# VectorE's add of two weight quarters, moved behind the low parts of the next up product

## The chip, the cores and the metric

The kernel runs on one core of one Trainium2 chip. The metric is the time of one execution on the device, in microseconds; the median of three runs is 2432.49 us (2432.47 to 2432.61). A core has five engines that run side by side, each through its own list of instructions in order, and that wait for each other through semaphores: TensorE (PE: matmuls, and PEld, the loads of the stationary operand), VectorE (DVE), ScalarE (ACT), GpSimd (POOL) and SyncE (SP). Here SyncE and GpSimd mostly issue transfers (DMA). The order in which each engine's instructions stand is fixed when the program is built.

## The reference

A decoder trunk of two layers on 256 tokens with 2048 features. Layer 0 mixes with a gated linear recurrence (HGRN2), layer 1 with an attention whose keys decay. Behind each mixer stands the MLP, which this change touches, and then a gated embedding:

```python
def sq_relu_mlp(u, w_up, w_down):
    hid = jax.nn.relu(u @ w_up)
    return (hid * hid) @ w_down

h = h + sq_relu_mlp(rms_norm(h, mlp_norm[layer]), w_mlp_up[layer], w_mlp_down[layer])
```

`w_up` is 2048 x 8192, `w_down` 8192 x 2048, all in float32. A changed order of work changes none of it.

## The kernel before

Each float32 factor is split into a high part, rounded to the 32-bit format that TensorE multiplies at full rate, and a low part, the rest. A product is three matmuls: high by high, high by low, low by high. Activations are split once. Weights come from memory into one of three buffers `raw` (1 MB each, `load_slab`, loaded by SyncE), and `split` makes the parts, 1024 columns at a time: ScalarE casts the high part `whi` (line 113), VectorE subtracts for the low part `wlo` (line 114). There are four buffers of each, used in turn; one is free when TensorE has done with it. `split` notes its last subtraction under the name "lo" in `order`, and `behind(ins, "lo")` tells the scheduler that `ins` must stand behind that subtraction on its engine, without a wait.

The MLP (`mlp`) goes through the 8192 hidden features in eight blocks b of 1024. `up(b, i)` makes 128 of them: 48 matmuls of 256 columns into a PSUM tile `ps`, with the slab of `w_up` as the weights; then ReLU and scale on VectorE (`scr`, line 304), a square on ScalarE (line 306), and the split of the result into `hid` (lines 237, 238). For the second four of a block, sums and differences of quarters of the hidden tile are made too (`sf`, lines 317 to 322).

`down(b)` multiplies a block with `w_down` by a scheme of seven products in place of eight: the hidden tile and the weights are cut in two by two quarters (features by tokens, features by columns), sums of quarters are multiplied, and the results `acc` are combined at the end. It does this for two sets of columns. The larger set's products are `p1` to `p7`; the smaller set's are `r1` to `r7`, with the running weight sum in the buffer `chq` (128 x 1536), and two products, `m0` and `m1`, cover the remaining columns. In the smaller set `r1` uses a quarter and `r5` the sum with a second one that the transfer adds. `r3` adds the buffer `cq` (line 436). `r6` multiplies that sum. `r2` loads another quarter into a `raw` buffer, multiplies it, and adds it to `chq` (line 429): this is the smaller set's last weight sum. `r4` splits and multiplies the result, and `r7` uses `cq`. The products `p` and `r` are 9 or 12 matmuls of 512 columns into PSUM, `pp` when the result is then added to `acc` by VectorE (line 338; copied by ScalarE in the first block, line 336), `pn` when a bank (`nbank`) gathers it over all blocks.

The list in line 467 sets the order of the products: for each block b from 1, eight `up(b, n)` with the products of `down(b - 1)` between them, ending in `up r6 r2 up r4 r7`. `Line` chains all matmuls of the MLP in that order on TensorE. The other engines' lists are laid out by a scheduler that places each instruction by an estimate of when its inputs are there, except where `behind` binds it. Behind the last block the results are combined (lines 477, 480), transposed (line 508) and added to the residual; the last block's second half is multiplied plainly, with weights loaded on line 514.

Of the kernel before, what the change touches and what calls it, by code (L numbers as in the profile page):

```python
# [14 lines left out]
ALU = mybir.AluOpType  # L15
# [20 lines left out]
def yoco_kernel(ctx, tc, a, out):  # L36
    nc = tc.nc
# [50 lines left out]
    def load_slab(src, n, parts, before=None):  # L88

        raw = wp.tile([P, D], F32, name="raw", tag="raw", bufs=3)  # L90
        m = n // parts
        if not before:
            nc.sync.dma_start(raw[:, :n], src)
        got = []
        for i in range(parts):
            r = raw[:, i * m : (i + 1) * m]
            if before:
                before[i]()
                nc.sync.dma_start(r, src[:, i * m : (i + 1) * m])
            got.append(split(r, m))  # L100
        return got
# [3 lines left out]
    def behind(ins, name):  # L105

        tc.add_manual_dep(ins.ins, order[name].name, mybir.DependencyInfo(mybir.DependencyClass.NoSync, mybir.DependencyReason.DATA), reason="order")

    def split(r, m, to=None, **dims):
        hi = wp.tile([P, 1024], F32R, name="whi", tag="whi", bufs=4)  # L110
        lo = wp.tile([P, 1024], F32R, name="wlo", tag="wlo", bufs=4)
        h_, l_ = (x[:, :m].rearrange(to, **dims) if to else x[:, :m] for x in (hi, lo))
        nc.scalar.copy(h_, r)  # L113
        order["lo"] = nc.vector.tensor_tensor(l_, r, h_.bitcast(F32), op=ALU.subtract).ins  # L114
        return hi, lo

    def wk(pair, k, lo):
        return pair[lo][:, k * P : (k + 1) * P]
# [17 lines left out]
    def mm_split(pairs, act, kcs=KC, off=0, ps=None, mm=nc.tensor.matmul):  # L136
        if ps is None:
            ps = psm.tile([P, T], F32, name="ps", tag="mm")
        for k in range(kcs):
            kk = k + off  # L140
            pair, kl = pairs[kk // 8], kk % 8
            st, sp = k == 0, k == kcs - 1
            mm(ps, wk(pair, kl, 0), act[:, k, 0, :], start=st, stop=False)  # L143
            mm(ps, wk(pair, kl, 0), act[:, k, 1, :], start=False, stop=False)  # L144
            mm(ps, wk(pair, kl, 1), act[:, k, 0, :], start=False, stop=sp)  # L145
        return ps
# [103 lines left out]
    def mlp(layer, u, stats, slots, u2, g2, pool, pps):  # L250
# [21 lines left out]
        chq = pool.tile([P, 1536], F32, name="chq", tag="chq", bufs=1)  # L272
# [15 lines left out]

        scr = pool.tile([P, 3 * T], F32, name="scr", tag="scr", bufs=1)
        squares = pool.tile([P, 2, T], F32, name="sqrs", tag="sqrs", bufs=1)  # L290
        def up(b, i):

            n = i // 2 + i % 2 * 4
            if n == 0:
                f = slot_flat(slots[b % 2], f"hid{layer}_{b}", 0 if b == NBL - 1 else 24)
                nf = f[:, : 8 * 2 * T].rearrange("p (k w t) -> p k w t", w=2, t=T)
                sf = f[:, 8 * 2 * T :].rearrange("p (j f w t) -> p j f w t", j=4, f=4, w=2)
                hid[b] = nf, sf
            nf, sf = hid[b]
            ps = mm_split(load_slab(a["w_up"][layer, b * 8 + n], D, 2), u, mm=line)  # L300
            if not rs:
                rs.append(stats.rstd())
            t = scr[:, :T]
            nc.vector.scalar_tensor_tensor(t, ps, 0.0, rs[0], op0=ALU.max, op1=ALU.mult)
            s = squares[:, i % 2, :]
            nc.scalar.activation(s, t, AF.Square)
            plain_split(nf, n, s)
            if b == NBL - 1:
                return
            if n < 4:  # L310
                return

            x = scr[:, T:].rearrange("p (f t) -> p f t", f=4)
            a11, a12 = (squares[:, i, :P] for i in range(2))
            a21 = squares[:, 0, P:].unsqueeze(1).broadcast_to([P, 2, P])
            both = squares.rearrange("p i t -> p (i t)").rearrange("p (g t) -> p g t", t=P)[:, 0::3]
            nc.vector.tensor_tensor(x[:, 0:2], a21, both, op=ALU.subtract)
            nc.vector.tensor_tensor(x[:, 2], a11, x[:, 1], op=ALU.subtract)
            nc.vector.tensor_tensor(x[:, 3], a12, x[:, 2], op=ALU.subtract)
            o = sf[:, n - 4]  # L320
            nc.scalar.copy(o[:, :, 0, :], x)
            nc.vector.tensor_tensor(o[:, :, 1, :], x, o[:, :, 0, :].bitcast(F32), op=ALU.subtract)
# [44 lines left out]
        def down(b):  # L367

            nf, sf = hid[b]

            def plain(half, tok):
                return lambda j: tuple(nf[:, 4 * half + j, w, tok * P : (tok + 1) * P] for w in range(2))

            def form(i):
                return lambda j: tuple(sf[:, j, i, w, :] for w in range(2))

            def one(name, op, pairs):
                o = psm.tile([P, 512], F32, name="pp", tag="mm")
                product(o, op, pairs, True)
                into(name, o)  # L380

            last = b == NBL - 2
            add = dict(accum_op=ALU.add)

            def p1():
                load(nc.gpsimd, cA, quarter(b, 0, 0))
                load(nc.gpsimd, cB, quarter(b, 1, 4))
                pairs = halves(cA)
                load(nc.gpsimd, cA, quarter(b, 0, 4), **add)
                one("1", plain(0, 0), pairs)  # L390

            def p3():
                one("3", form(S4), halves(cB))

            def p2():
                one("2", plain(1, 0), loaded(quarter(b, 1, 0)))

            def p5():
                one("5", form(S1), halves(cA))

                for i in range(2):
                    v, w = (x.rearrange("p (n k c) -> p k n c", n=4, k=4)[:, 2 * i : 2 * i + 2] for x in (cA, cB))
                    nc.vector.tensor_tensor(v, v, w, op=ALU.add)
                load(nc.gpsimd, cB, quarter(b, 0, 4), **add)

            def p7():
                one("7", form(S3), halves(cB))
                load(nc.gpsimd, cq, quarter(b, 1, 12, f=fr))

            def p6():  # L410
                pairs = halves(cA)
                load(nc.gpsimd, cA, quarter(b, 1, 0), **add)
                one("6", form(S2), pairs)

            def p4():
                one("4", plain(1, 1), halves(cA))

            def r1():
                load(nc.gpsimd, chq, quarter(b, 0, 8, f=fr))
                pairs = chunks(chq, 3)  # L420
                load(nc.gpsimd, chq, quarter(b, 0, 12, f=fr), **add)
                one("r1", plain(0, 0), pairs)

            def r2():
                r = raw_tile()[:, :1536]
                load(nc.sync, r, quarter(b, 1, 8, f=fr))
                product(nbank[0][0], plain(1, 0), chunks(r, 3), False, last)

                behind(nc.vector.tensor_tensor(chq, chq, r, op=ALU.add), "lo")  # L429

            def r5():
                one("r5", form(S1), chunks(chq, 3))

            def r3():
                product(nbank[1][0], form(S4), chunks(cq, 3), False, last)
                behind(nc.vector.tensor_tensor(chq, chq, cq, op=ALU.add), "lo")
                load(nc.gpsimd, cq, quarter(b, 0, 12, f=fr), **add)

            def r6():
                one("r6", form(S2), chunks(chq, 3))  # L440

            def r4():
                product(nbank[0][1], plain(1, 1), chunks(chq, 3), False, last)

            def r7():
                one("r7", form(S3), chunks(cq, 3))

            def m(q):

                raw = raw_tile()[:, :1024]  # L450
                load(nc.sync, raw, quarter(b, q, 8, 8, fm))
                hi, lo = split(raw, 1024)
                for c in range(2):
                    cols = slice(c * 512, (c + 1) * 512)
                    for t in range(2):

                        product(nbank[c][t], lambda j: plain(q, t)(3), [(hi[:, cols], lo[:, cols])], b == q == 0, last and q == c == t == 1)

            return dict(p1=p1, p2=p2, p3=p3, p4=p4, p5=p5, p6=p6, p7=p7, r1=r1, r2=r2, r3=r3,
                        r4=r4, r5=r5, r6=r6, r7=r7, m0=lambda: m(0), m1=lambda: m(1))  # L460

# [379 lines left out]
    late = ctx.enter_context(tc.tile_pool(name="late", bufs=1))  # L841
# [245 lines left out]
```

## Time and profile before

| what | value |
| --- | --- |
| median of three runs | 2432.49 us |
| the profiled execution, its own time | 2432.98 us |
| its span (first to last instruction) | 2431.2 us |
| TensorE: matmuls / weight loads | 2404.9 us (99%) / 2285.2 us (94%) |
| VectorE / ScalarE / GpSimd busy | 1937.2 us (80%) / 1474.8 us (61%) / 157.9 us (6%) |
| granted clock of TensorE, mean | 0.997 |
| one block of an MLP (sum to sum) | 83.76 us |

In rows of the profile a number such as L114 is a line of the kernel; `out<-in` gives tiles by name. A timeline row gives start, length, engine, line, operation, tiles, shapes and how many were merged; the bracket behind it gives how long the engine had been idle before it and what ended that. A row of waits gives the total, how often and the longest. Rows of one engine may overlap a little, since the next instruction starts while the end of the last one is still on its way. In a merged row of two, the length goes from the first one's start to the last one's end.

### The profile page before, as it was taken

How to read it: one execution, taken by the hardware profiler on the slowest of the kernel's cores; microseconds unless marked ns; L12 is line 12 of the kernel's file. 1: busy time of each engine (PE TensorE's matmuls, PEld its weight loads, DVE VectorE, ACT ScalarE, POOL GpSimd, SP SyncE). 2: the span in 40 equal slices, each digit the busy share in tenths (PEclk: the TensorE clock that was granted, in tenths of full speed). 3: DMA queues.
4: the chain of work that ended last, by engine and by line, in shares of the span. 5: the costliest groups of instructions: out<-in, count | busy, mean ns of one | idle time of the engine just before them, and what ended most of it. 6: DMA issues, size and time to landing. Idle time of an engine off the chain costs nothing.

```text
span 2431.2 us, 43771 instructions
## 1 busy us (share of the span) xinstructions
PE 2404.9 (99%) x17898; PEld 2285.2 (94%) x17898; DVE 1937.2 (80%) x2914; ACT 1474.8 (61%) x2224; POOL 157.9 (6%) x201
## 2 busy tenths in 40 slices
PE   9999999999999999999999999999999999999998
PEld 8999999999999999899999999999999999989998
DVE  7897797678888888889874566667888888888976
ACT  6666575566666666656664555556666666665664
POOL 1000000001110111110000000000011011111000
PEclk9999999999999999999999999999999999999999
DMA  6554545578888887886555655557888888788653
GB/s 243 175 182 174 186 179 208 196 235 250 231 226 243 239 230 234 251 213 230 189 184 183 206 178 179 180 196 246 237 232 235 241 246 219 237 246 225 226 191 122
DMA packets 148985, 518.07 MB, mean 213 GB/s; under 512 B 9136, under 2 KB 59888, under 8 KB 111408
## 3 DMA queue, kind: packets, MB, share of 16 engines
q1 hardware_dynamic: 95200, 382.62, 44.2%
q0 software_dynamic: 52288, 130.62, 23.6%
q8 instruction: 140, 2.29, 0.4%
q10 hardware_dynamic: 1296, 2.03, 0.2%
q14 instruction: 61, 0.50, 0.1%
HBM read 508.91 MB, written 6.32 MB: 212 GB/s over the span
## 4 chain that ended last, share of the span: by engine, by line
PE 96%; DVE 2%; issue 1%; ACT 0%; DMA 0%; POOL 0%; DVEq 0%; POOLq 0%
PE ps L131 29%; PE pp L131 15%; PE ps L143 12%; PE ps L145 12%; PE ps L144 12%; PE pst L131 7%; PE pn L131 6%; DVE wlo L114 1%; DVE chq L429 0%; ACT whi L113 0%; PE pu L143 0%; PE pu L144 0%; PE pu L145 0%; DVE accr L338 0%; PE pa L741 0%
## 5 line engine op out<-in xcount | busy, mean ns | idle before, releaser
L113 ACT CAST whi<-raw 128x1024 fp32r<-128x1024 f32 (+2 forms) x742 | 763.3, 1033 | 667.9 <-PE ps L144 280.1
L114 DVE TENSOR_TENSOR wlo<-raw,whi 128x1024 fp32r<-128x1024 f32 (+2 forms) x742 | 886.6, 1200 | 329.2 <-ACT whi L113 323.5
L131 PE MATMUL ps<-u_m,whi 128*128 128x256 f32 x4096 | 707.3, 276 | 0.0
L131 PEld LDWEIGHTS ps<-u_m,whi 128*128 128x128 f32 x4096 | 626.0, 188 | 8.7
L131 PE MATMUL ps<-u_m,wlo 128*128 128x256 f32 x2048 | 566.4, 277 | 9.0 <-DVE wlo L114 8.8
L131 PEld LDWEIGHTS ps<-u_m,wlo 128*128 128x128 f32 x2048 | 384.6, 188 | 11.8 <-DVE wlo L114 11.8
L131 PE MATMUL pp<-whi,hid 128*128 128x512 f32 x1120 | 364.1, 390 | 0.0
L113 ACT CAST whi<-chain 128x1024 fp32r<-128x1024 f32 x224 | 221.1, 997 | 137.6 <-PE ps L131 89.2
L114 DVE TENSOR_TENSOR wlo<-chain,whi 128x1024 fp32r<-128x1024 f32 x224 | 256.7, 1156 | 28.4 <-ACT whi L113 26.8
L131 PEld LDWEIGHTS pp<-whi,hid 128*128 128x128 f32 x1120 | 210.2, 188 | 41.3
L131 PE MATMUL pp<-wlo,hid 128*128 128x512 f32 x560 | 218.5, 390 | 0.0
L143 PE MATMUL ps<-u_a,whi 128*128 128x256 f32 x768 | 213.6, 278 | 0.0
L145 PE MATMUL ps<-u_a,wlo 128*128 128x256 f32 x768 | 211.9, 276 | 0.0
L144 PE MATMUL ps<-u_a,whi 128*128 128x256 f32 x768 | 211.9, 276 | 0.0
L131 PE MATMUL pn<-whi,hid 128*128 128x512 f32 x476 | 158.2, 390 | 0.0
L283 POOL DMA_DIRECT2D chain<-in_w_down x98 | 104.0, 1061 | 749.7 <-DVE wlo L114 302.3
L143 PEld LDWEIGHTS ps<-u_a,whi 128*128 128x128 f32 x768 | 144.3, 188 | 0.2
L144 PEld LDWEIGHTS ps<-u_a,whi 128*128 128x128 f32 x768 | 144.3, 188 | 0.2
L145 PEld LDWEIGHTS ps<-u_a,wlo 128*128 128x128 f32 x768 | 144.2, 188 | 0.1
L143 PE MATMUL ps<-u_p,whi 128*128 128x256 f32 x512 | 141.2, 276 | 0.0
L145 PE MATMUL ps<-u_p,wlo 128*128 128x256 f32 x512 | 140.9, 275 | 0.0
L144 PE MATMUL ps<-u_p,whi 128*128 128x256 f32 x512 | 140.9, 275 | 0.0
(294 smaller groups left out, 4712.7 us busy)
## 6 DMA issues: line engine op xcount, KB each, us to landing
raw<-in_w_up SPq DMA_DIRECT2D x128, 1024.0 KB, 5.6
chain<-in_w_down POOLq DMA_DIRECT2D x70, 1024.0 KB, 9.4
raw<-in_w_ain SPq DMA_DIRECT2D x48, 1024.0 KB, 4.8
raw<-in_w_pg SPq DMA_DIRECT2D x32, 1024.0 KB, 4.8
raw<-in_w_down SPq DMA_DIRECT2D x30, 1024.0 KB, 5.4
chq<-in_w_down POOLq DMA_DIRECT2D x28, 768.0 KB, 6.5
chain<-in_w_down POOLq DMA_DIRECT2D x28, 768.0 KB, 6.5
raw<-in_w_vf SPq DMA_DIRECT2D x20, 832.0 KB, 4.4
```

What stands on the lines that cost most here:

```text
L113: nc.scalar.copy(h_, r)
L114: order["lo"] = nc.vector.tensor_tensor(l_, r, h_.bitcast(F32), op=ALU.subtract).ins
L131: ins = nc.tensor.matmul(*args, **kw).ins
L143: mm(ps, wk(pair, kl, 0), act[:, k, 0, :], start=st, stop=False)
L144: mm(ps, wk(pair, kl, 0), act[:, k, 1, :], start=False, stop=False)
L145: mm(ps, wk(pair, kl, 1), act[:, k, 0, :], start=False, stop=sp)
L283: eng.dma_start(dst.rearrange("p (n f) -> p n f", f=src.shape[-1]), src, **kw)
```

## The change

The sum on line 429 is no longer issued inside `r2`. `r2` puts it on a list, `late`, and the next `up` issues it once the up product's slab has been split and its matmuls have been issued. It is still bound behind the last low part, which now is the second low part of that up's slab. `r4`, which reads the sum, still comes after that up.

```diff
         scr = pool.tile([P, 3 * T], F32, name="scr", tag="scr", bufs=1)
         squares = pool.tile([P, 2, T], F32, name="sqrs", tag="sqrs", bufs=1)
+        late = []
+
         def up(b, i):
...
             ps = mm_split(load_slab(a["w_up"][layer, b * 8 + n], D, 2), u, mm=line)
+            while late:
+                late.pop()()
             if not rs:
                 rs.append(stats.rstd())
...
                 product(nbank[0][0], plain(1, 0), chunks(r, 3), False, last)
 
-                behind(nc.vector.tensor_tensor(chq, chq, r, op=ALU.add), "lo")
+                late.append(lambda: behind(nc.vector.tensor_tensor(chq, chq, r, op=ALU.add), "lo"))
```

Four lines come in ahead, so line 429 is line 433 in the changed kernel, and 304, 338, 317, 508 are 308, 342, 321, 512. How VectorE's list stands between `r2` and `r7` in the second block of the first MLP: before,

```order
L114 TENSOR_TENSOR wlo<-raw,whi 128x512
L429 TENSOR_TENSOR chq<-chq,raw 128x1536
L238 TENSOR_TENSOR hid_2_7569<-sqrs,hid_2_7569 128x256
L338 TENSOR_TENSOR accr_7442<-accr_7442,pp 128x512
L114 TENSOR_TENSOR wlo<-raw,whi 128x1024 x2
L114 TENSOR_TENSOR wlo<-chq,whi 128x1024
L114 TENSOR_TENSOR wlo<-chq,whi 128x512
L114 TENSOR_TENSOR wlo<-chain,whi 128x1024
L304 SCALAR_TENSOR_TENSOR scr<-ps,rstd 128x256
L114 TENSOR_TENSOR wlo<-chain,whi 128x512
L317 TENSOR_TENSOR scr<-sqrs 128x256
```

and in the changed kernel (the 128x512 low part from `raw` is the end of `r2`'s weights, the two 128x1024 ones are the up slab's; `chq` is `r4`'s, `chain` is `r7`'s):

```order
L114 TENSOR_TENSOR wlo<-raw,whi 128x512
L238 TENSOR_TENSOR hid_2_7569<-sqrs,hid_2_7569 128x256
L342 TENSOR_TENSOR accr_7442<-accr_7442,pp 128x512
L114 TENSOR_TENSOR wlo<-raw,whi 128x1024 x2
L433 TENSOR_TENSOR chq<-chq,raw 128x1536
L114 TENSOR_TENSOR wlo<-chq,whi 128x1024
L114 TENSOR_TENSOR wlo<-chq,whi 128x512
L308 SCALAR_TENSOR_TENSOR scr<-ps,rstd 128x256
L114 TENSOR_TENSOR wlo<-chain,whi 128x1024
L114 TENSOR_TENSOR wlo<-chain,whi 128x512
L321 TENSOR_TENSOR scr<-sqrs 128x256
```

The sum now stands behind the up slab's two low parts, and the ReLU of that up (`scr`) now stands ahead of both low parts of `r7`. In the last block of each MLP the scheduler also places the first four transposes of the results elsewhere on TensorE. Before, they stand inside `r7` (`pp`), behind `r4` (`pn`):

```order
L131 MATMUL pn_6166<-whi,hid_6_11005 128x512
L131 MATMUL pp<-whi,hid_6_11005 128x512
L508 MATMUL ptr<-ident,acc_7231 128x128
L508 MATMUL ptr<-ident,acc_7254 128x128
L508 MATMUL ptr<-ident,acc_7231 128x128
L508 MATMUL ptr<-ident,acc_7254 128x128
L131 MATMUL pp<-wlo,hid_6_11005 128x512
```

and in the changed kernel behind the last up (`ps`), ahead of `r4`:

```order
L131 MATMUL ps<-u_m_5112,wlo 128x256
L512 MATMUL ptr<-ident,acc_7231 128x128
L512 MATMUL ptr<-ident,acc_7254 128x128
L512 MATMUL ptr<-ident,acc_7231 128x128
L512 MATMUL ptr<-ident,acc_7254 128x128
L131 MATMUL pn_6166<-whi,hid_6_11005 128x512
L131 MATMUL pn_6166<-wlo,hid_6_11005 128x512
```

The four transposes pass the nine matmuls of `r4` and the first of `r7`. In that block VectorE's list also has a final sum (line 477 before) between the two low parts of the up slab, and two more (lines 480 and 477) between the moved sum and `r4`'s low parts. The lists of SyncE and GpSimd are the same in both kernels.

## The prediction

> **The bound.** I read the page first, then TensorE's waits, then single rows around one of the moved sums. The page's first part (busy time, share of the span, instructions) and the chain that ended last, by engine:
>
> ```profile
> PE 2404.9 (99%) x17898; PEld 2285.2 (94%) x17898; DVE 1937.2 (80%) x2914; ACT 1474.8 (61%) x2224; POOL 157.9 (6%) x201
> PE 96%; DVE 2%; issue 1%; ACT 0%; DMA 0%; POOL 0%; DVEq 0%; POOLq 0%
> ```
>
> TensorE is the bound, and VectorE (DVE) has 2% of the chain: some 49 us through which the chain runs over VectorE, though TensorE was busy during most of it. What counts is how long TensorE stood. The waits of TensorE, products and weight loads (total us, times, longest), the summed rows of line 429, and one block of the first MLP from one sum to the next (length, then busy time of PE, PEld, DVE, ACT, POOL):
>
> ```profile
> PE ps L131 <- DVE wlo L114: 8.8, 12, 0.7
> PEld ps L131 <- DVE wlo L114: 11.8, 14, 0.9
> ...
> L429 DVE TENSOR_TENSOR chq<-chq,raw x14: 1750/1751/1753, 599.3 to 2258.2; 128x1536 f32<-128x1536 f32 x14
> ...
> 682.50:766.26 83.76, 83.03 (x556) 76.01 (x556) 73.76 (x94) 52.16 (x67) 9.46 (x9) 1.00 0.84 236
> ```
>
> Fourteen weight loads of an up product waited for a low part, and there are fourteen sums on line 429. In a block of 83.76 us TensorE is idle for 0.73 us, and that is one of these waits. So the block holds one hole, and the rest of it is full at a granted clock of 1.00.
>
> The hole, in the second block, in order of time on TensorE (r6 is pp, r2 pn, up ps; then r4 pn, r7 pp, the next up), with the weight load that waits:
>
> ```profile
> 681.16 0.40 PE L131 MATMUL pp<-whi,hid 128*128 128x512 f32 x1
> ...
> 683.00 0.39 PE L131 MATMUL pp<-whi,hid 128*128 128x512 f32 x1
> ...
> 685.26 0.39 PE L131 MATMUL ps<-u_m,whi 128*128 128x256 f32 x2
> 686.38 0.19 PEld L131 LDWEIGHTS ps<-u_m,wlo 128*128 128x128 f32 x1 [0.93 <-DVE wlo L114]
> 686.39 0.38 PE L131 MATMUL ps<-u_m,wlo 128*128 128x256 f32 x1 [0.73 <-DVE wlo L114]
> ...
> 691.75 0.40 PE L131 MATMUL pn<-whi,hid 128*128 128x512 f32 x1
> ...
> 693.80 0.39 PE L131 MATMUL pp<-whi,hid 128*128 128x512 f32 x1
> ...
> 695.84 0.39 PE L131 MATMUL ps<-u_m,whi 128*128 128x256 f32 x2
> ```
>
> And VectorE and ScalarE (ACT) in the same place:
>
> ```profile
> 681.90 0.69 DVE L114 TENSOR_TENSOR wlo<-raw,whi 128x512 fp32r<-128x512 f32 x1
> 682.51 1.75 DVE L429 TENSOR_TENSOR chq<-chq,raw 128x1536 f32<-128x1536 f32 x1
> 684.18 0.42 DVE L238 TENSOR_TENSOR hid<-sqrs,hid 128x256 fp32r<-128x256 f32 x1
> 684.51 0.68 DVE L338 TENSOR_TENSOR accr<-accr,pp 128x512 f32<-128x512 f32 x1
> 685.11 2.36 DVE L114 TENSOR_TENSOR wlo<-raw,whi 128x1024 fp32r<-128x1024 f32 x2
> 687.38 1.82 DVE L114 TENSOR_TENSOR wlo<-chq,whi 128x1024 fp32r<-128x1024 f32 x2
> ...
> 691.95 0.42 DVE L304 SCALAR_TENSOR_TENSOR scr<-ps,rstd 128x256 f32<-128x256 f32 x1 [0.53 <-PE ps L131]
> ...
> 682.27 0.41 ACT L237 CAST hid<-sqrs 128x256 fp32r<-128x256 f32 x1
> 682.74 2.01 ACT L113 CAST whi<-raw 128x1024 fp32r<-128x1024 f32 x2
> 684.78 1.57 ACT L113 CAST whi<-chq 128x1024 fp32r<-128x1024 f32 x2
> ...
> 693.32 2.01 ACT L113 CAST whi<-raw 128x1024 fp32r<-128x1024 f32 x2
> ```
>
> VectorE runs without a gap from 681.90 to the low parts. The high part of the up slab is cast from 682.74, yet its low part starts only at 685.11, behind the sum (1.67 us from its start to the next start), the low part of the hidden tile (0.33) and the accumulation of r6 (0.60).
>
> **Its price.** The up product takes 691.75 - 685.26 = 6.49 us. An undisturbed one, and the ends of the one in the first block (where r6 is copied by ScalarE and no accumulation stands in front):
>
> ```profile
> 668.31 5.48 PE ps L131 x48
> ...
> 602.09 0.39 PE L131 MATMUL ps<-u_m,whi 128*128 128x256 f32 x2
> ...
> 607.99 0.40 PE L131 MATMUL pn<-whi,hid 128*128 128x512 f32 x1
> ```
>
> So a hole costs 6.49 - 5.48 = 1.01 us in a block with the accumulation (twelve, six in each MLP), and 5.90 - 5.48 = 0.42 us in each MLP's first block (two). Sum: 12 x 1.01 + 2 x 0.42 = 12.96 us. That is all that can be won here.
>
> **The change.** No instruction is added or removed: the fourteen sums of 1.75 us stay. Three things move.
>
> *The low parts go ahead of the sum.* In the new order VectorE has, behind the 0.69 us low part of r2: hidden low part, accumulation, two low parts of up, the sum. The hidden low part can start when its cast ends, 682.27 + 0.41 = 682.68, so at about 682.71. The accumulation needs r6's last matmul, 683.00 + 0.39 = 683.39; the hand-over took 0.04 us at the hole (685.11 + 1.23 = 686.34 to 686.38), so it starts at 683.43. The first low part follows 0.60 later at 684.03, ends at 685.26 and is seen at 685.30. The waiting weight load was ready at 686.38 - 0.93 = 685.45. So the hole closes with 0.15 us to spare. That is thin; a shortfall of 0.1 us in each of twelve blocks would cost 1.2 us, plus a little for the restart. Bounds: nothing is left of the hole, or half of it (0.5 us, if the accumulation gets its PSUM bank later than I think). I take 0.02 a block, near the computed end: 0.3 us in all. In the first blocks there is no accumulation and the margin is wider. The low part's own lower limit, the cast's end at 682.74 + 1.05, does not bind.
>
> *The sum, and what hangs on it, comes later.* The second low part starts 1.13 us behind the first (2.36 - 1.23), the sum at 686.30; it ends at 688.05 instead of 684.26. Then ScalarE's cast of chq (about 1.05) to 689.13, and its low part to 690.39. r4 now starts at 691.75 - 1.01 = 690.74 and wants the first low part with its second matmul, 0.23 later (2.05 us for nine), at 690.97. Cover: 0.58 us, where it was 3.4 us before (687.38 + 1.23 against 691.75 + 0.23). If the cover went, each 0.1 us beyond it costs 1.4 us over fourteen blocks.
>
> *Behind that on VectorE,* the ReLU of up (scr) now stands ahead of r7's two low parts. It waits for the end of up, 691.95 - 1.01 = 690.94, when VectorE is just free; r7's first low part runs 691.27 to 692.50, wanted at 693.80 - 1.01 + 0.23 = 693.02. Then 0.69, 0.42, and the next up's first low part, whose cast (693.32 - 1.01) ends at 693.36: about 693.40 to 694.63, wanted at 695.84 - 1.01 + 0.19 = 695.02. Margins of 0.5 and 0.4 us; no new hole.
>
> **Queues.** The sum is the last reader of r2's raw tile, so the load that takes that slot (the weights of the second up after it) goes out later. SyncE's wait for the sum, the issue, its cast, and the time to landing of raw loads in this block (660 to 720 us) and in the whole span:
>
> ```profile
> SPq L93 <- DVE chq L429: 94.8, 12, 7.9
> SPq L514 <- DVE chq L429: 15.2, 2, 7.6
> ...
> 684.33 3.50 SPq L93 DMA_DIRECT2D raw<-in_w_up  x2
> ...
> 698.69 1.06 ACT L113 CAST whi<-raw 128x1024 fp32r<-128x1024 f32 x1 [0.94 <-PE ps L131]
> ...
> DMA to landing us min/median/max: 3.9/7.4/7.9
> ...
> DMA to landing us min/median/max: 3.6/4.8/12.1
> ```
>
> Issue moves from 684.33 to 688.12; with 7.4 to 7.9 us it lands by 696.0, and the cast is due at 697.68. TensorE needs that slab at 694.83 + 5.48 + 2.73 = 703.04 (an up and the twelve matmuls of p1), so landing by 700.7 is enough (1.05 of cast, 1.23 of low part). Cost zero. The loads queued behind it on SyncE (one at about 687.5 in the old run) shift by under a microsecond. GpSimd's next chq load waits for the end of r4's low parts, which moves from 687.38 + 1.82 = 689.20 to about 690.98; its data is wanted two ups and two products after r7, as r1. Cost zero.
>
> **Last blocks.** The last block of each MLP has final sums between, and four transposes move ahead of r4:
>
> ```profile
> 1105.20 0.38 PE L131 MATMUL ps<-u_m,wlo 128*128 128x256 f32 x1 [0.73 <-DVE wlo L114]
> 1106.20 0.68 DVE L477 TENSOR_TENSOR accr<-accr,accr 128x512 f32<-128x512 f32 x1
> 1108.54 0.68 DVE L480 TENSOR_TENSOR accr<-pn,accr 128x512 f32<-128x512 f32 x1
> 1112.87 0.60 PE L508 MATMUL ptr<-ident,acc 128*128 128x128 f32 x4
> ```
>
> It is the second block plus 418.81 us. One 0.60 us step goes between the two low parts, so the sum ends at 1107.46 and the cast at 1108.54; two steps of 0.60 follow the sum, and chq's first low part ends at 1109.81. The transposes read PSUM bank pn00 freed by the L480 step (about 1108.1), so they run at 1109.55 for 0.35 us, and r4 wants its low part at 1110.13. No wait. Their cost is only moved. The two L514 loads behind the sum feed products that start some 10 us later. Cost zero, with 1 us either way.
>
> **Sum.** 2432.49 - 12.96 + 0.3 = 2419.8 us. The profiled execution took 2432.98 with a span of 2431.2, so 1.8 us lie around the span and it stands 0.5 above the median; its span should become about 2418.5.
>
> **Rivals.**
>
> *A: VectorE's steps do not overlap.* If each step began only when the one before had ended, the margins shrink: first low part seen at 685.38 (still in time), chq's at 690.66, the ReLU ends at 691.77, r7's low part is 0.02 late, and the next up's ends at 695.34, 0.36 late. Twelve times 0.36 is 4.3: 2423.8 us. Against it: 684.18 + 0.42 is 684.60, and the next row starts at 684.51; the rows overlap by 0.09 throughout. The Trainium skill, "VectorE: DVE Perf Modes", section "The DRAIN you can't avoid", has it this way: a next step does not begin until the pipe is empty. By that rule this rival would hold; these rows speak for earlier starts. 7%.
>
> *B: the accumulation is late and half the hole stays:* 12 x 0.5 = 6 us back, 2425.8. For it: no row here shows an accumulation waiting on pp, only the 0.04 of other hand-overs. 5%.
>
> *C: the low parts are held by their ring of four buffers, not by the sum,* and the hole stays: 2432.5. Against it: their buffers were r6's, last read by TensorE before 683.4, and VectorE had no idle time ahead of 685.11. The Trainium skill, "Perfetto Trace Analysis", section "Identifying the Most-Contended Engine", says that a gap which repeats can mean too few buffers; by that rule nothing would change, but the rows name VectorE's queue. 4%.
>
> *D, slower: the later load becomes the bound.* Place: the raw slot that the sum frees. From 12.6 us to landing (700.7 - 688.12) TensorE waits, from 13.6 the block is slower than before. At 15 us: 14 x 2.4 - 13 = 20.6 us, 2453. Against it: 7.9 here, 12.1 the longest anywhere. 4%.
>
> **Numbers.** Forecast 80%: 2419.8, between 2418.4 (another 0.1 a block that the holes cost in restarts) and 2422. A ends within 2424.0, which I take as the upper end. About 0.2%, 4.9 us, is what this measurement can tell from no change; A and B still lie beyond it. Faster 80 + 7 + 5 = 92%, less 1 for a shortfall that I do not see; within it C and that one, 5%; slower D, 4%.
>
> **Signs.** Right: TensorE's waits for low parts in the MLP blocks gone, a block of 82.75 us instead of 83.76, the accumulation's row at about 1.1 us earlier than now, chq's low part ending within 0.6 us before r4. Wrong: a wait on the first or second matmul of r4 or r7 (the sum too late), on the next up's low part (A), or a raw cast that waits for a DMA (D).

## The result

The changed kernel takes 2419.90 us in the median of five runs (2419.56 to 2420.65), the kernel before, beside it, 2432.47 us (2431.91 to 2432.61): a ratio of 0.9949, 95% interval 0.9935 to 0.9964. That is 12.6 us less. Its profiled span is 2418.2 us, 13.0 us under the old one.

The page of the changed kernel, busy time and chain by engine:

```profile
PE 2401.8 (99%) x17898; PEld 2284.9 (94%) x17898; DVE 1934.8 (80%) x2914; ACT 1472.1 (61%) x2224; POOL 157.9 (7%) x201
PE 99%; DVE 0%; DMA 0%; ACT 0%; issue 0%; POOL 0%; DVEq 0%; POOLq 0%
```

VectorE's 2% of the chain are gone. The weight loads of the low parts, in the groups by line (busy, mean ns, idle time before and its releaser), of before:

```profile
L131 PEld LDWEIGHTS ps<-u_m,wlo 128*128 128x128 f32 x2048 | 384.6, 188 | 11.8 <-DVE wlo L114 11.8
```

and of the changed kernel, with a block of the first MLP from sum to sum:

```profile
L131 PEld LDWEIGHTS ps<-u_m,wlo 128*128 128x128 f32 x2048 | 384.6, 188 | 0.0
...
685.88:768.64 82.76, 82.76 (x557) 75.94 (x556) 73.57 (x94) 51.95 (x66) 9.45 (x9) 1.00 0.85 238
```

All fourteen waits are gone, and TensorE is busy for the whole 82.76 us of the block, which was 83.76 before. The first matmul of the first MLP and the first of the embedding behind it, before:

```profile
484.92 0.39 PE L131 MATMUL ps<-u_m,whi 128*128 128x256 f32 x2
...
1161.98 0.28 PE L143 MATMUL pu<-pt,whi 128*128 128x256 f32 x1
```

and in the changed kernel:

```profile
484.91 0.39 PE L131 MATMUL ps<-u_m,whi 128*128 128x256 f32 x2
...
1155.48 0.28 PE L143 MATMUL pu<-pt,whi 128*128 128x256 f32 x1
```

This MLP went from 677.06 to 670.57 us, 6.49 less. The second one, between the same two instructions, went from 677.08 to 670.57. So both together give 13.0 us, and the rest of the program is as it was.

The second block of the changed kernel, TensorE, in order of time:

```profile
680.75 0.40 PE L131 MATMUL pp<-whi,hid 128*128 128x512 f32 x1
...
684.85 0.39 PE L131 MATMUL ps<-u_m,whi 128*128 128x256 f32 x2
684.96 0.19 PEld L131 LDWEIGHTS ps<-u_m,wlo 128*128 128x128 f32 x1
685.08 0.28 PE L131 MATMUL ps<-u_m,wlo 128*128 128x256 f32 x1
...
690.33 0.40 PE L131 MATMUL pn<-whi,hid 128*128 128x512 f32 x1
690.33 0.19 PEld L131 LDWEIGHTS pn<-wlo,hid 128*128 128x128 f32 x1
690.56 0.39 PE L131 MATMUL pn<-wlo,hid 128*128 128x512 f32 x1
```

and VectorE, ScalarE and SyncE there:

```profile
683.01 0.69 DVE L342 TENSOR_TENSOR accr<-accr,pp 128x512 f32<-128x512 f32 x1 [0.28 <-PE pp L131]
683.61 2.35 DVE L114 TENSOR_TENSOR wlo<-raw,whi 128x1024 fp32r<-128x1024 f32 x2
685.88 1.75 DVE L433 TENSOR_TENSOR chq<-chq,raw 128x1536 f32<-128x1536 f32 x1
688.81 1.83 DVE L114 TENSOR_TENSOR wlo<-chq,whi 128x1024 fp32r<-128x1024 f32 x2 [1.18 <-ACT whi L113]
690.55 0.42 DVE L308 SCALAR_TENSOR_TENSOR scr<-ps,rstd 128x256 f32<-128x256 f32 x1
690.89 1.82 DVE L114 TENSOR_TENSOR wlo<-chain,whi 128x1024 fp32r<-128x1024 f32 x2
...
693.04 1.23 DVE L114 TENSOR_TENSOR wlo<-raw,whi 128x1024 fp32r<-128x1024 f32 x1
...
697.27 1.06 ACT L113 CAST whi<-raw 128x1024 fp32r<-128x1024 f32 x1 [1.11 <-PE ps L131]
...
685.99 2.00 SPq L93 DMA_DIRECT2D raw<-in_w_up  x2
```

The block runs 0.41 us earlier than in the old trace (680.75 against 681.16). The first low part now ends at 683.61 + 1.23 = 684.84, and its weight load runs at 684.96 without a wait. VectorE's new idle time, 1.18 us for ScalarE's cast of chq, stands where nobody waits for it.

### The profile page after: what moved, and what is told of

Its sections match the earlier page's. It is cut to its first block, busy times and chain, and to the rows that moved or that the text cites. A ratio compares the mean times of both kernels' runs of the same rounds, so it can differ in the third digit from the quotient of the medians.

```text
span 2418.2 us, 43787 instructions
## 1 busy us (share of the span) xinstructions
PE 2401.8 (99%) x17898; PEld 2284.9 (94%) x17898; DVE 1934.8 (80%) x2914; ACT 1472.1 (61%) x2224; POOL 157.9 (7%) x201
## 4 chain that ended last, share of the span: by engine, by line
PE 99%; DVE 0%; DMA 0%; ACT 0%; issue 0%; POOL 0%; DVEq 0%; POOLq 0%
PE ps L131 29%; PE pp L131 16%; PE ps L143 12%; PE ps L145 12%; PE ps L144 12%; PE pst L131 8%; PE pn L131 7%; PE pu L145 0%; PE pu L144 0%; PE pu L143 0%; PE pa L745 0%; PE ptr L512 0%; PE pl L951 0%; DMA lbl<-in_lb 0%; PE ptp L974 0%; DVE h L1024 0%
## 5 line engine op out<-in xcount | busy, mean ns | idle before, releaser
L113 ACT CAST whi<-chq 128x1024 fp32r<-128x1024 f32 x112 | 92.2, 837 | 99.2 <-PE ps L131 74.1
L143 PE MATMUL ps<-u_p,whi 128*128 128x256 f32 x512 | 141.2, 276 | 0.0
```

## The experiments

The kernel before stood beside every one (2432.5 to 2432.8 us). Where a fraction of a microsecond counts, the length of one block, sum to sum, is compared; the whole time also holds the first stage, whose length until the first MLP differs between the traces by up to 1.4 us (483.9 to 485.3), and what stands behind the second MLP, which differs by up to 0.9 us (111.9 to 112.8).

**The accumulation moved in the sum's place** (on the kernel before, with the list `late` of the change):

```diff
     else:
-        nc.vector.tensor_tensor(acc[name], acc[name], ps, op=ALU.add)
+        def add():
+            return nc.vector.tensor_tensor(acc[name], acc[name], ps, op=ALU.add)
+        if name == "r6":
+            late.append(lambda: behind(add(), "lo"))   # issued in the next up, as in the change
+        else:
+            add()
```

> The kernel before, with the sum left in front, but the accumulation of r6 (0.60 us from start to start) moved behind the up slab's low parts in its place. Queue theory: in the twelve blocks that have an accumulation the hole shrinks by 0.60 us, from 1.01 to about 0.4; the two first blocks keep 0.42. 12 x 0.60 = 7.2 us less than the kernel before: about 2425.2 us, and fourteen waits of about 0.3 us are left. Theory that the sum itself does it (its data, its raw buffer or its load): no change, 2432.5 us. Buffer theory: no change.

Measured: 2425.27 us, ratio 0.9969 (0.9958 to 0.9981), 7.2 us less. Its wait rows and a block:

```profile
PEld ps L131 <- DVE wlo L114: 4.7, 14, 0.3
...
681.52:764.70 83.18, 83.05 (x556) 76.02 (x555) 73.75 (x94) 52.16 (x67) 9.46 (x9) 1.00 0.84 237
```

Fourteen waits of 0.3 us are left, and a block is 0.58 us shorter. The sum stands where it stood, the buffers, its data and its load are as before, and the hole shrinks by the time of the step that left the front. This rules out both the buffers and the sum's data as the cause: what counted was VectorE's time in front of the low parts.

**The front doubled, and half of that** (on the kernel before; the up slab's low parts are kept behind both steps):

```diff
-                behind(nc.vector.tensor_tensor(chq, chq, r, op=ALU.add), "lo")
+                behind(nc.vector.tensor_tensor(chq, chq, chq, op=ALU.max), "lo")   # 768 columns in the second
+                s = nc.vector.tensor_tensor(chq, chq, r, op=ALU.add)
+                behind(s, "lo")
+                order["front"] = s.ins      # later low parts are put behind this
```

> The kernel before, with a second step of the same size as the sum (maximum of chq with itself, which leaves chq as it is) on VectorE ahead of the sum, and both ahead of the up slab's low parts. Queue theory (a hole is the time that VectorE's list takes in front of the low parts): each of the fourteen holes grows by one such step, 1.67 us from start to start, so 14 x 1.67 = 23.4 us more than the kernel before, about 2455.8 us; the waits for low parts go from 0.93 to about 2.6 us each. Buffer theory (the low parts wait for their ring of four buffers): no change, 2432.5 us.

> The kernel before with a second step of half the sum's width (768 columns) on VectorE ahead of the sum, both ahead of the up slab's low parts: holes of about 1.6 us of idle TensorE, between the 0.73 us of the kernel before and the 2.40 us of the doubled sum, behind half of which the granted clock fell. Queue theory alone: 0.87 us from start to start in each of fourteen blocks, 12.2 us above the kernel before, about 2444.7 us, a block of 84.6 us and a granted clock of 1.00 in every stretch. If a hole of 1.6 us already lets the clock fall in half of the blocks: 7 x 1.5 = 10.5 us more, about 2455 us, with blocks of 86.1 us among them.

Measured: 2464.89 us with the full step, ratio 1.0130 (1.0117 to 1.0144), 32.4 us more and not 23.4; 2444.88 us with half of it, ratio 1.0049 (1.0032 to 1.0066), 12.1 us more. The waits and one block with half a step:

```profile
PE ps L134 <- DVE wlo L114: 21.2, 14, 1.6
...
685.14:769.79 84.65, 83.05 (x556) 76.03 (x556) 74.62 (x95) 52.23 (x67) 9.46 (x9) 1.00 0.82 233
```

and with the full one: its waits, three of its blocks (the first is the first block of the first MLP), the matmuls behind the holes of the first and the third of them, and 5 us from near the end of the latter hole:

```profile
PE ps L134 <- DVE wlo L114: 32.4, 14, 2.4
...
600.52:687.59 87.07, 85.27 (x560) 78.13 (x559) 74.90 (x95) 53.34 (x68) 9.48 (x9) 0.98 0.80 227
687.59:773.04 85.45, 83.05 (x557) 76.03 (x556) 75.42 (x96) 52.16 (x66) 9.46 (x9) 1.00 0.83 231
1857.85:1944.68 86.83, 84.43 (x557) 77.41 (x556) 75.42 (x95) 52.16 (x66) 9.47 (x9) 0.98 0.80 227
...
603.46 0.38 PE L134 MATMUL ps<-u_m,wlo 128*128 128x256 f32 x1 [1.80 <-DVE wlo L114]
1860.79 0.58 PE L134 MATMUL ps<-u_m,wlo 128*128 128x256 f32 x1 [2.40 <-DVE wlo L114]
...
1860.00:1865.00 5.00, 4.21 (x24) 4.21 (x25) 3.61 (x4) 1.35 (x3) 0.77 (x1) 0.66 0.86 301
```

A block grows by 0.89 with half a step and by 1.69 with a full one (0.87 and 1.67 were expected): the hole follows VectorE's time in front, step for step. The rest of the full step's loss, some 9 us in the median, is another thing. In seven blocks of the traced run, the first one of the first MLP and the first six of the second, the granted clock falls behind the hole. The holes are not all alike: in the two first blocks, without an accumulation, TensorE idles for 1.8 us, in the other twelve for 2.4 us. Both holes of 1.8 us cost clock, and five of the twelve of 2.4 us; a block with one of these five is longer by some 1.5 us (86.83 to 87.05 against 85.45). With half a step the holes are 1.0 us in the two first blocks and 1.6 us in the others, and no block lost clock. Only one of the full step's four runs was traced. They lie 5.1 us apart (2461.39 to 2466.5), so the number of such blocks may differ from run to run.

**The last block left as before** (on the changed kernel):

```diff
+                if last:
+                    late.pop()()
```

> The changed kernel, but in the last block of each MLP the sum stays in front as before; the transposes stand again inside r7. If the transposes' new place and the final sums cost nothing, as forecast: two holes of 1.01 us come back, 2.0 us above the changed kernel, about 2421.9 us. If the last block's new order costs something that the closed holes hide: less than 2.0 us above it, or below it.

Measured: 2421.14 us, ratio 0.9953 (0.9940 to 0.9967), 1.2 us above the changed kernel's median, where 2.0 were expected. Its waits:

```profile
PE ps L131 <- DVE wlo L114: 1.5, 2, 0.7
```

Two holes are back. From the first matmul of the first MLP to the embedding this kernel needs 1156.03 - 484.40 = 671.63 us, 1.06 more than the changed one, and as much more in the second MLP: 2.1 us in all. What is missing in the whole time lies outside the MLPs: the first stage is 0.5 us shorter in this trace, and the part behind the second MLP 0.4 us. So the last block gains its 1.0 us like the others, and the transposes in their new place cost nothing that these traces resolve.

**A small step in front** (on the changed kernel; `front` is taken up by the next up slab's low parts):

```diff
+                if name == "r6":
+                    w = acc[name][:, :256]
+                    front.append(nc.vector.tensor_tensor(w, w, w, op=ALU.max).ins)
```

> The changed kernel with a small step on VectorE (256 columns, 0.33 us from start to start) between the accumulation of r6 and the up slab's low parts. Margin of the low part in the changed kernel by its profile: due at 684.96, seen at 684.87, so 0.09 us. Queue theory: 0.33 - 0.09 = 0.24 us late, with 0.1 of restart 0.34 at most, in twelve blocks: 3 to 4 us above the changed kernel, 2423 to 2424 us. If the low parts had room (the raw cast or a buffer were what they wait for): no change, 2419.9 us.

Measured: 2425.18 us, ratio 0.9968 (0.9955 to 0.9980), 5.3 us above the changed kernel instead of 3 to 4. VectorE, the waits and a block:

```profile
683.37 0.69 DVE L349 TENSOR_TENSOR accr<-accr,pp 128x512 f32<-128x512 f32 x1 [0.28 <-PE pp L134]
684.09 0.42 DVE L352 TENSOR_TENSOR accr<-accr 128x256 f32<-128x256 f32 x1
684.43 2.35 DVE L114 TENSOR_TENSOR wlo<-raw,whi 128x1024 fp32r<-128x1024 f32 x2
...
PEld ps L134 <- DVE wlo L114: 3.8, 12, 0.4
...
686.70:769.84 83.14, 83.04 (x557) 76.01 (x557) 73.91 (x96) 52.03 (x66) 9.45 (x9) 1.00 0.84 237
```

The holes come back in twelve blocks, each 0.38 us longer, so the low parts have almost no room. The step cost more than its own 0.33 us: it reads what the accumulation writes and starts 0.03 us behind that one's end (683.37 + 0.69 = 684.06), 0.72 behind its start, where the low part in the changed kernel starts 0.60 behind. The 0.12 us more makes 0.45, less 0.08 of margin 0.37. The 0.7 us that the whole time has beyond 12 x 0.38 is of the size of the differences outside the MLPs.

**The cover behind the sum** (on the changed kernel, a step on chq behind the sum, once full, once 256 columns):

```diff
+                def sums():
+                    behind(nc.vector.tensor_tensor(chq, chq, r, op=ALU.add), "lo")
+                    behind(nc.vector.tensor_tensor(chq, chq, chq, op=ALU.max), "lo")   # or [:, :256]
+                late.append(sums)
```

> The changed kernel with a second step of the sum's size (1.67 us from start to start; maximum of chq with itself) on VectorE behind the sum, so that chq is ready that much later; the ReLU of up then stands ahead of r4's low parts. Cover theory (0.53 us are left between r4's first low part, ready at 690.03, and its second matmul at 690.56): the cast runs 689.3 to 690.4, the low part, behind the ReLU, ends at about 692.1: r4 is 1.6 us late in each of fourteen blocks, 22 us above the changed kernel, 2441 to 2444 us, with waits of pn for low parts that the changed kernel does not have. If the up product covered the sum widely: no change, 2419.9 us.

> The changed kernel with a small step (256 columns, 0.33 us) on VectorE behind the sum. Cover theory: r4's low part ends 0.3 us later, at 690.3, still ahead of 690.56, so r4 does not wait; behind it the ReLU, r7's low parts and the next up's first low part come 0.3 us later, and that last one had 0.23 us to spare, so it may be 0.1 to 0.2 us late: 0 to 2.5 us above the changed kernel, 2419.9 to 2422.4 us. If no cover were left: 14 x 0.33 = 4.6 us, 2424.5 us.

Measured with the full step: 2447.44 us, ratio 1.0063 (1.0047 to 1.0079), 27.5 us above the changed kernel; 22 were expected. Its waits, VectorE and a block:

```profile
PE pn L131 <- DVE wlo L114: 13.5, 14, 1.0
PE pn L131 <- ACT whi L113: 3.2, 4, 1.4
...
691.64 0.42 DVE L308 SCALAR_TENSOR_TENSOR scr<-ps,rstd 128x256 f32<-128x256 f32 x1 [1.09 <-PE ps L131]
691.99 1.82 DVE L114 TENSOR_TENSOR wlo<-chq,whi 128x1024 fp32r<-128x1024 f32 x2
...
687.00:771.52 84.52, 83.36 (x557) 76.08 (x556) 75.25 (x96) 52.11 (x66) 9.45 (x9) 1.00 0.83 234
```

r4 waits in all fourteen blocks, and a block is 1.76 us longer than the changed kernel's; VectorE idles for 1.09 us and then does the ReLU ahead of the low part that r4 wants. This is the kernel slower than before: with the sum too late for the up product to cover, moving it loses more than the holes were worth. Seven such blocks make 12.3 us; the two MLPs are 13.5 and 13.4 us longer than in the changed kernel, so their last blocks lose about 1 us more.

Measured with 256 columns: 2424.33 us, ratio 0.9968 (0.9956 to 0.9981), 4.4 us above the changed kernel; at most 2.5 were expected. The waits, VectorE and r4 in a middle block, that block, and the chain in the last block of the first MLP:

```profile
PE pn L131 <- DVE wlo L114: 1.5, 2, 0.8
...
686.96 0.42 DVE L435 TENSOR_TENSOR chq<-chq 128x256 f32<-128x256 f32 x1
688.56 1.83 DVE L114 TENSOR_TENSOR wlo<-chq,whi 128x1024 fp32r<-128x1024 f32 x2 [1.18 <-ACT whi L113]
...
689.62 0.40 PE L131 MATMUL pn<-whi,hid 128*128 128x512 f32 x1
689.84 0.19 PEld L131 LDWEIGHTS pn<-wlo,hid 128*128 128x128 f32 x1
...
685.17:768.13 82.96, 82.96 (x557) 75.91 (x556) 73.81 (x96) 51.92 (x66) 9.46 (x9) 1.00 0.84 238
...
1104.60 0.42 DVE scr L308
1105.02 1.22 DVE wlo L114
...
1106.29 2.13 PE pn L131 x8
```

The middle block loses 0.20 us, with no wait listed. The cover was shorter than the expectation had it, because the low part is read by the weight load and not by the matmul. In the changed kernel this weight load runs together with r4's first matmul (both at 690.33), 0.23 us ahead of the second matmul (690.56). The low part, ready at 690.03 and seen 0.04 later, so had 0.26 us to spare and not 0.53. And the step costs more than 0.33 us: it reads what the sum writes and starts 0.04 us behind the sum's end (685.17 + 1.75 = 686.92), so chq's low part stands 3.39 us behind the sum's start (688.56 against 685.17) where it stood 2.93 behind it (688.81 against 685.88). That is 0.46 us later, less 0.26 of margin 0.20. The rows agree: the low part ends at 689.78, and its weight load runs at 689.84, 0.22 us behind r4's first matmul.

In the last block the ReLU had been placed ahead of r4's low part, and r4 waited; the same happened in the second MLP (two waits of up to 0.8 us in the list). The expectation had the order of the middle blocks in mind for all of them. The MLPs are 2.65 and 2.76 us longer than in the changed kernel; six blocks of 0.20 us leave some 1.5 us for the last block of each.

## Why the prediction was right

*The bound and the hole's price.* 12.96 us were to be won; the two MLPs are 13.0 us shorter (6.49 and 6.51), a block 1.00 us. The price of 1.01, which is more than the 0.73 or 0.93 that the wait rows show, came from the length of the up product and held.

*The low part in front.* The accumulation was put at 683.43 in old time, so at 683.02 in this trace's; it ran at 683.01. It waited for r6's last matmul, as forecast, and rival B (half a hole left by it) did not come. The spare time was forecast as 0.15 us; 684.84 + 0.04 against 684.96 leaves 0.08. The old weight load's wait had been counted from 685.45, and without a hole it would have been due at 685.37 by the new rows, so that term was mis-sized by 0.08. The allowance of 0.3 us for a late low part was not needed.

*The cover behind the sum.* Forecast: chq's first low part 0.58 us ahead of r4's second matmul. It ended at 688.81 + 1.22 = 690.03 against 690.56, 0.53. But the forecast measured to the wrong row: the weight load of that matmul needs the low part first, and it runs at 690.33, with r4's first matmul (in the old trace too it runs at 691.75, where r4 starts). So 0.30 us were left, 0.26 behind the hand-over, and not 0.58. The two runs with a later sum show that this cover is real and as short as that. The 0.5 us of margin that the forecast gave r7's first low part is too long by the same 0.23. For up the forecast did go by the weight load: the next up's first low part ended at 694.27, its weight load due at 694.54.

*The load.* The prediction had the load into the sum's slot go out at 688.12 in old time, 687.7 in this one. There are two loads here: one at 685.99, when the low parts had ended, before the sum's end at 687.63, and one at 685.99 + 2.00 - 0.33 = 687.66 behind it. So the load needed first no longer waits for the sum, which the prediction missed. SyncE's wait for the sum shrank:

```profile
SPq L93 <- DVE chq L433: 15.1, 12, 1.3
```

It was 94.8 us before. The cast at 697.27 waits for TensorE and not for a transfer, so the cost of zero held. Two casts elsewhere wait for a transfer of `w_down` as none did before (1.47 us at 785.33, in the first MLP; 1.83 us at 1119.72, behind its last up). The second is the sign that the prediction had set for rival D, but TensorE waits behind neither, so D's cost did not come.

*The last blocks* cost nothing, as forecast, by the run with the last block left as before.

*Rival A* (VectorE's steps do not overlap) did not hold for this order: the low part was in time (684.84 against 684.96), so were the later ones, and low parts start 0.60 us behind a 0.69 us accumulation. The run with a small step in front shows the one case in which it is right: a step that reads what the one before it wrote. The section "The DRAIN you can't avoid" of the Trainium skill's page "VectorE: DVE Perf Modes", which the prediction drew on for this rival, also says that a next step which is not held starts earlier; the rows of independent steps agree with that, with starts about 0.08 us before the reported end. So the rule as a whole did not speak for this rival.

*Rival C* (buffers) fell with the moved accumulation. What the prediction took for it from the Trainium skill's page "Perfetto Trace Analysis" stands there in the section "Optimization Strategy": a gap that repeats can mean too few buffers. Here the repeating gap came from the order of VectorE's list.

The forecast of 2419.8 us stands against 2419.90, within the 1.1 us that the five runs spread. The range was 2418.4 to 2424.0. The mechanism and the price of the holes are borne out by the traces. That the medians agree to 0.1 us is luck: the traces' gain of 13.0 us is 0.3 above the forecast one, and the parts outside the MLPs differ by more than that from trace to trace.

## What to carry to other kernels

Where the engine that sets the end waits in short, equal holes, look at what stands in front of the awaited step in the list of the engine that makes it, and move something whose result is wanted later, whichever step that is. The hole costs more than its wait row shows: compare the length of the stretch with and without it. Then work out the new due time of the moved step, since the cover that it gets is a fixed length, and count it up to the weight load that reads the result, not up to the matmul: here 0.3 us were left of it, and a second step of 1.7 us behind the sum turned the gain of 13 us into a loss of 15.

## What the runs showed of the hardware

Holes of 1.8 and 2.4 us on TensorE lowered the granted clock behind them in seven of fourteen places of one traced run: behind both holes of 1.8 us and behind five of the twelve of 2.4 us. In one stretch of 5 us, from the end of a hole of 2.4 us on, the mean was 0.66, and blocks with such a loss took some 1.5 us more than those with the same hole that kept the clock. Holes of 1.6 us did this in none of twelve. The Trainium skill, "TensorE: Matmul & The Clock Gate", section "What's actually happening", gives an idle window of about 3.4 us for the fall to half rate; here 1.8 us of idle time was enough both times, and 2.4 us in five of twelve cases. What decides it, these runs do not show.

On VectorE a step that does not need the one before it starts about 0.08 us before that one's end (690.89 against 690.55 + 0.42 = 690.97); one that reads its result starts 0.03 to 0.04 us behind the end (684.09 against 684.06, 686.96 against 686.92). In a tight place, who depends on whom is worth 0.12 us a step.
